# Values of the dilated attention for four head slots in one pass, two slots' values parked in memory

## The chip, the cores and the metric

The kernel runs on one core of a Trainium2 chip. The metric is the device time of one execution in microseconds (us). Of the kernel before, three runs are known: 2054.96, 2056.84 and 2059.21 us, median 2056.84.

## The reference

Two decoder layers over 1024 tokens of 1024 features, in float32. The first layer normalises its input, projects it, and runs three branches: a gated linear recurrence, a dilated attention, and an attention to 256 memory tokens. The second layer is a sparse attention, and this change does not touch it.

The dilated attention has three groups (dilation 1, 4 and 16) of four heads each, 128 features per head. A query of group g sees keys at stride d. The four heads of one group have the same place in the other groups, a "slot", and a slot's three outputs are mixed by their softmax sums:

```
w = jax.nn.softmax(jnp.stack(lses, axis=0), axis=0)
o = jnp.einsum('gbsh,gbshd->bshd', w, jnp.stack(outs, axis=0).astype(jnp.float32))
```

The values v are a plain projection of the normalised input, with 512 columns per group (four slots of 128).

## The kernel before, in words

Every large product is made exact with three matmuls: both operands are split into a high and a low part (high*high, high*low, low*high). The input lies feature-major in eight chunks of 128 features by 1024 tokens, each as a high and a low tile (`self.xt`, `xh` and `xl`).

Weights come as a stream in an order written out by hand (`self.plan`, filled in `layer1`). Each piece is 512 KB. `w()` (L187) hands out piece i, and before that issues the load of piece i+2 on SP's queue and the split of piece i+1: POOL writes the high part (L215), VectorE the low part (L216). Raw, high and low parts share a ring of six buffers (`NW`), so piece i+1's high part takes the buffer of piece i-1's, and can only be written when the matmuls of piece i-1 are done; the load of piece i+2 takes the buffer of raw piece i, and waits for its split.

`proj` (L223) makes a feature-major product: 48 matmuls of 512 columns per piece, with the weights stationary. Queries and keys are made so, one piece per group and slot, and VectorE brings them out of PSUM (L519) in the group's token order.

The values must be token-major, so `dil_vals` (L602) has the input as the stationary operand. `seq_block` (L560) picks its 128 tokens in the group's order: adjacent columns for group 0, every 4th for group 1, every 8th for group 2. The moving operand is 256 weight columns, the values of two slots. One call does one group and two slots: two pieces of four feature chunks each, and for each piece 2 (PSUM tiles) x 4 (token blocks) x 4 (chunks) x 3 matmuls, so 192 matmuls of 256 columns (L613). Each PSUM tile (two banks, `big`, two of them) collects four token blocks; VectorE scales it and writes one tile per slot (L621). `dil_slot` (L740) calls it for the three groups in slot 0 (for slots 0 and 1) and again in slot 2 (for slots 2 and 3): six calls in all.

Scores, mixing weights and outputs of a slot are side work: generators whose steps are woven in by `tick`, called once per six 512-column matmuls of `proj`, and once per token block in `dil_vals` (16 ticks a call). A slot's scores have 12 steps, the mix 3, the output 14; the preparation of the memory operands has 25 steps at the start and 12 when slot 2 begins. The memory attention takes every second tick while it runs. The steps of the memory branch are counted by `next(extra)`, and `M1`, `M2` say at which count its keys and values are made; `M2` is the start of slot 3.

Working tiles of 4 KB per partition come from one ring of 39 (`NU`): the split input holds 16 of them, the values 6.

Of the kernel before, what the change touches and what calls it, by code (L numbers as in the profile page):

```python
# [31 lines left out]
M1, M2, MS = 8, 30, 2  # L32
# [18 lines left out]
class Trunk:  # L51
# [46 lines left out]
    def psum_layout(self, wide):  # L98
        """Four banks as two tiles of two banks, or as three score banks and a third for transposes."""
        if self.wide is not None:  # L100
            self.bs.close()
        self.wide, self.banks, self.fills = wide, 0, 0
        self.bs = ExitStack()
        self.bp = self.bs.enter_context(self.tc.tile_pool(name=self.n("bp"), bufs=1, space=PSUM))
# [25 lines left out]
    def chain(self):  # L130
        """The instruction just made follows the chain's last one (same engine, order only)."""
        cur = self.nc.cur_f.blocks[-1].instructions[-1]
        if self.chained is not None:
            info = mybir.DependencyInfo(mybir.DependencyClass.NoSync, mybir.DependencyReason.SCHED_ONLY)
            self.tc.add_manual_dep(cur, self.chained, info, reason="order")
        self.chained = cur.name

    def order_allocations(self):
        """Tiles of a shared ring take their buffers in the order in which they are first written."""
        first, pos = {}, {}  # L140
        want = {nm for names in self.rings.values() for nm in names}
        for blk in self.nc.cur_f.blocks:
            for ins in blk.instructions:
                for o in getattr(ins, "outs", ()):
                    bap = getattr(o, "bass_ap", None)
                    nm = getattr(getattr(bap, "tensor", None), "name", None)
                    if nm in want and nm not in first:
                        pos[nm] = len(first)
                        first[nm] = ins
        info = mybir.DependencyInfo(mybir.DependencyClass.NoSync, mybir.DependencyReason.SCHED_ONLY)  # L150
        for names in self.rings.values():
            prev = None
            for nm in sorted(names, key=pos.get):
                cur = first[nm]
                if prev is not None and prev.name != cur.name:
                    self.tc.add_manual_dep(cur, prev.name, info, reason="ring order")
                prev = cur

# [28 lines left out]
    def w(self):  # L187
        """Next piece of the planned weight stream as exact (high, low) parts."""
        i = self.pos
        self.pos += 1  # L190
        self.prefetch(i + 3, i + 2)
        r = self.split_w[i]
        self.split_w[i] = None
        return r
# [28 lines left out]
    def proj(self, x, halves=(0, 1)):  # L223
        """Feature-major product: 128 output features against the tokens of the given halves."""
        w = self.w()
        ps = self.big()
        for k in range(8):
            self.proj_step(ps, w, x, k, halves)
            if x[k][0][0].shape[-1] == 512 or k % 4 == 3:
                self.tick()  # L230
        return ps
# [16 lines left out]
    def rstd_steps(self, ssum, nb, p=None):  # L248
        """Columns 1/sqrt(mean+eps) of nb token blocks from per-feature-lane sums of squares."""
# [39 lines left out]
    def split_x(self, src, k, gcol, cuts):  # L289
        """Gain-scaled split operand of feature chunk k, by token halves."""  # L290
# [10 lines left out]
    def split_halves(self, src, k, gcol):  # L301
        """The same with a buffer of its own for each half."""
# [23 lines left out]
    def mem_prep(self, gcol):  # L326
        """Normalised memory, scaled with a layer's gain and split."""
# [25 lines left out]
    def mem_norm(self, raw):  # L353
        """Rows of the memory tokens' 1/rms, the same for both layers."""
# [39 lines left out]
    def mem_kv(self, gcol):  # L394
        """Split keys and values of one layer: each key part fills both partition halves."""
# [35 lines left out]
    def mem_attn(self, q, kv, done, pause=0):  # L431
        """q: two pairs of split heads [2 parts x 64, tokens], already scaled; done(c, out) takes each output."""
# [75 lines left out]
    def dil_proj(self, x, row, g, sc):  # L508
        """Projection scaled and put into the group's sequence order."""
# [16 lines left out]
    def dil_scores(self, D, g, q, k):  # L526
        """Probability numerators of one group with their minima of -s and sums."""
# [32 lines left out]
    def seq_block(self, t, g, m):  # L560
        """Block m of 128 tokens in a group's sequence order."""
# [7 lines left out]
    def to_seq(self, T, fs, out):  # L569
        """Columns of token blocks brought into the order of the second and third group."""  # L570
# [25 lines left out]
    def dil_cols(self, col):  # L596
        """Columns of the norm's factors in each group's order."""
# [4 lines left out]
    def dil_vals(self, g):  # L602
        """Token-major values of a group for two slots."""
        nc = self.nc
        pss = [self.big(), self.big()]
        for kh in range(2):
            h, l = self.w()
            for i, ps in enumerate(pss):
                for b in range(4):
                    for k in range(4):  # L610
                        xh, xl = (self.seq_block(t, g, 4 * i + b) for t in self.xt[4 * kh + k])
                        for j, (x, w) in enumerate(((xh, h), (xh, l), (xl, h))):
                            nc.tensor.matmul(ps[:, 256 * b:256 * b + 256], x, w[:, k, :],  # L613
                                             start=(kh == k == j == b % 2 == 0), stop=(kh == 1 and k == 3 and j == 2),
                                             skip_group_check=True)
                    self.tick()
                if kh:
                    if i == 0:
                        out = [self.u("dv", F32, (128, 8, 128)) for _ in range(2)]
                    for e, v in enumerate(out):  # L620
                        nc.vector.tensor_tensor(v[:, 4 * i:4 * i + 4, :],  # L621
                                                ps.rearrange("p (b s n) -> p s b n", b=4, s=2)[:, e],
                                                self.dcol[g][:, 4 * i:4 * i + 4, None].to_broadcast([128, 4, 128]),
                                                op=ALU.mult)
        return out

    def dil_mix(self, D):
        """Weights of the three groups' numerators, in each group's own order."""
# [111 lines left out]
    def dil_slot(self, s, x, row, extra):  # L740
# [9 lines left out]
        if s % 2 == 0:  # L750
            self.vals = []
            for g in range(3):
                self.vals.append(self.dil_vals(g))
                next(extra)
                next(extra)
        D["v"] = self.vals
        self.add_side(self.dil_out(D))

# [90 lines left out]
    def z_gate(self, i, x, row):  # L849
        """Output chunk i times silu of its gate, v/2 (1 + tanh(v/2))."""  # L850
# [16 lines left out]
    def layer1(self):  # L867
# [5 lines left out]
        for j in range(36):  # L873
            p, i = divmod(j, 18)
            vals = 6 <= i < 12
            if not vals:
                self.pieces(a["hw_dil"][12 * p + i - 6 * (i >= 12)], tile=None if j else self.u)
            elif i % 2 == 0:
                self.pieces(*(a["hw_dv"][6 * p + i - 6 + t] for t in range(2)))
            if not vals:  # L880
                self.pieces(*mem.get(j, ()))
            elif i % 2:
# [130 lines left out]
    def out_proj(self, order, res, done, last=None):  # L1013
        """Feature-major output chunks with the residual added."""
# [39 lines left out]
    def split_pair(self, half, p):  # L1054
        """Two gated feature chunks of a token half as (high, low) parts."""
# [13 lines left out]
    def out_half(self, res):  # L1069
        """Output chunks of the first token half, the residual, and the final norm."""  # L1070
# [48 lines left out]
    def out_tail(self, res):  # L1119
        """The same for the second half, with the last chunk and the norm by quarters."""  # L1120
# [93 lines left out]
    def nsa_group(self, seg):  # L1214
        """Split key operands of one group for the keys that a token half sees."""
# [65 lines left out]
    def cmp_split(self, t, pcol):  # L1281
        """The compression network's input blocks [(parity, d), position pair, (group, block)], split."""
# [95 lines left out]
    def nsa_cmp(self, it):  # L1378
        """Compressed-branch probabilities (transposed, split) and the block selection."""
# [53 lines left out]
    def nsa_query(self, it):  # L1433
        """Split query operands of eight heads with the position and selection rows."""
# [32 lines left out]
    def nsa_scores(self, W):  # L1467
        """Gated probabilities of one branch for two heads."""
# [44 lines left out]
    def nsa_apply(self, W):  # L1513
        """Transposed, split probabilities of one work; the products follow DELAY batches later."""
# [46 lines left out]
    def seg_load(self, seg):  # L1561
        """Operands of a segment (token half, group) that come from memory."""
# [187 lines left out]
    def z_half(self, ps, row, half, z):  # L1750
        """silu of a projected half: v/2 (1 + tanh(v/2))."""
# [7 lines left out]
    def fill_proj(self, x, row):  # L1759
        """Query and gate projections of the second token half."""  # L1760
# [119 lines left out]
def _layout(i):  # L1880
# [21 lines left out]
    for s in range(4):  # L1902
        for g in range(3):
# [3 lines left out]
            if s % 2 == 0:  # L1907
                b = 5120 + (g * 4 + s) * 128
                v = panel(w, r(b, b + 256))
                dv += [v[:, :4], v[:, 4:]]  # L1910
# [46 lines left out]
```

## Time and profile before

| | |
|---|---|
| median of three runs | 2056.84 us |
| profiled execution, first to last instruction (its span) | 2053.8 us |
| PE (matmul) busy | 1974.9 us, 96% |
| VectorE / ScalarE / GpSimd busy | 57% / 41% / 39% |
| DMA | 129.38 MB, mean 63 GB/s |

No time of the profiled execution is given apart from its span. A row of the profile gives the line of the kernel, the engine, the operation, the tiles (out<-in), the shapes and the count; then the busy time and the mean of one. PE is the matmul, PEld the load of its stationary operand, which has records of its own and runs beside the matmuls. The duration of a matmul is longer than its share of the stream, since matmuls are pipelined: the distance from one start to the next is what a matmul costs.

### The profile page before, as it was taken

The page shows a single profiled execution, that of the slowest core. Times are in us where ns is not written, and L with a number is a line of the kernel's source. Part 1 is how long each engine was busy: PE and PEld are TensorE (multiplying, and loading weights), DVE is VectorE, ACT ScalarE, POOL GpSimd, SP SyncE. Part 2 cuts the span into 40 slices and gives each one's busy share as a digit, 9 for nine tenths or more (in the row PEclk, how much of TensorE's full clock was granted, in tenths as well). Part 3 has the DMA queues.
Part 4 walks back from the last instruction along what each step waited for, and adds up shares of the span by engine and source line. Part 5 has one row for each costly group of instructions (what it writes and reads, how often), then busy time and mean ns, then how long its engine had stood idle before and what let it go on. Part 6 is the DMA issues. An engine that isn't in the chain of part 4 may idle for free. (4 is left out here: it accounts for less than half of the span.)

```text
span 2053.8 us, 28410 instructions
## 1 busy us (share of the span) xinstructions
PE 1974.9 (96%) x10594; PEld 1694.0 (82%) x10594; DVE 1166.5 (57%) x2257; ACT 839.8 (41%) x1780; POOL 810.6 (39%) x929
## 2 busy tenths in 40 slices
PE   8999999999999999999999999999999899998997
PEld 7899988889988777788888987778777788887886
DVE  6421255341133475656125466668778877889964
ACT  4210144220021272332005244246557766788861
POOL 6120112221011444441221533466677565577533
PEclk9999999999999999999999999999999999999999
DMA  4111111111112111113222332322222012311013
GB/s 176 42 32 42 52 31 32 52 32 31 31 42 72 32 41 42 42 44 132 76 72 75 101 121 72 112 72 73 62 83 93 18 52 77 99 54 48 12 47 102
DMA packets 53065, 129.38 MB, mean 63 GB/s; under 512 B 7872, under 2 KB 16576, under 8 KB 52928
## 3 DMA queue, kind: packets, MB, share of 16 engines
q1 hardware_dynamic: 52928, 127.57, 19.6%
q8 instruction: 84, 1.38, 0.3%
q14 instruction: 53, 0.43, 0.1%
HBM read 110.78 MB, written 16.78 MB: 62 GB/s over the span
## 5 line engine op out<-in xcount | busy, mean ns | idle before, releaser
L215 POOL TENSOR_SCALAR wh<-raw 128x1024 fp32r<-128x1024 f32 (+2 forms) x137 | 156.4, 1144 | 728.2 <-PE big L239 287.4
L216 DVE TENSOR_TENSOR wl<-raw,wh 128x1024 fp32r<-128x1024 f32 (+4 forms) x139 | 179.1, 1292 | 200.2 <-POOL wh L215 177.8
L1510 POOL TENSOR_SCALAR P<-P,nden,gates 128x640 f32<-128x640 f32 (+7 forms) x256 | 212.8, 841 | 136.0 <-DVE nden L1507 117.8
L239 PE MATMUL big<-xh,wh 128*128 128x512 f32 x752 | 258.4, 424 | 1.1 <-ACT xh L296 0.6
L239 PE MATMUL big<-xl,wh 128*128 128x512 f32 x752 | 242.8, 399 | 4.0 <-DVE xl L297 4.0
L239 PE MATMUL big<-xh,wl 128*128 128x512 f32 x752 | 234.0, 392 | 0.0
L1504 ACT ACTIVATE P<-P,nden 128x640 f32<-128x640 f32 (+7 forms) x256 | 187.5, 733 | 89.9 <-DVE nden L1502 84.4
L1528 DVE TENSOR_TENSOR pl<-t,ph 128x512 fp32r<-128x512 f32 (+1 forms) x304 | 183.2, 614 | 37.2 <-ACT ph L1527 33.5
L1523 PE MATMUL t<-ident,P 128*128 128x128 f32 x1056 | 167.8, 278 | 16.7 <-DVE pl L1528 13.6
L1527 ACT ACTIVATE ph<-t 128x512 fp32r<-128x512 f32 (+1 forms) x304 | 159.3, 533 | 58.8 <-PE t L1523 47.9
L239 PEld LDWEIGHTS big<-xl,wh 128*128 128x128 f32 x752 | 142.0, 189 | 35.3 <-DVE xl L297 5.4
L1523 PEld LDWEIGHTS t<-ident,P 128*128 128x128 f32 x1056 | 126.4, 142 | 50.5 <-DVE pl L1528 12.4
L239 PEld LDWEIGHTS big<-xh,wl 128*128 128x128 f32 x752 | 142.0, 189 | 30.4
L239 PEld LDWEIGHTS big<-xh,wh 128*128 128x128 f32 x752 | 135.2, 190 | 36.6 <-issue 15.1
L239 PE MATMUL big<-x,wh 128*128 128x512 f32 x480 | 144.4, 395 | 0.0
L613 PE MATMUL big<-wh,xh 128*128 128x256 f32 x384 | 140.5, 366 | 0.5 <-DVE kbd L411 0.5
L613 PE MATMUL big<-wl,xh 128*128 128x256 f32 x384 | 139.8, 364 | 0.0
L613 PE MATMUL big<-wh,xl 128*128 128x256 f32 x384 | 139.7, 364 | 0.0
L1549 PE MATMUL acc<-ph,nv 128*128 128x256 f32 x528 | 128.2, 310 | 6.0 <-ACT ph L1527 5.4
L1549 PE MATMUL acc<-pl,nv 128*128 128x256 f32 x528 | 122.3, 299 | 0.0
L1502 DVE CUSTOM_DVE_ANT_0 P<-big,mask 128x640 f32<-128x640 f32 (+3 forms) x128 | 116.7, 913 | 4.0 <-PE big L1493 2.5
L613 PEld LDWEIGHTS big<-wh,xh 128*128 128x128 f32 x384 | 109.7, 286 | 0.9 <-issue 0.7
(339 smaller groups left out, 4321.1 us busy)
## 6 DMA issues: line engine op xcount, KB each, us to landing
raw<-nw_f SPq DMA_DIRECT2D x42, 512.0 KB, 3.6
raw<-hw_dil SPq DMA_DIRECT2D x22, 512.0 KB, 3.6
raw<-now SPq DMA_DIRECT2D x32, 256.0 KB, 2.7
raw<-hw_z SPq DMA_DIRECT2D x14, 512.0 KB, 3.5
raw<-how SPq DMA_DIRECT2D x16, 448.0 KB, 3.4
raw<-hw_dv SPq DMA_DIRECT2D x12, 512.0 KB, 3.6
raw<-hw_xa SPq DMA_DIRECT2D x8, 512.0 KB, 3.6
res<-xT SPq DMA_DIRECT2D x8, 512.0 KB, 5.2
```

Of the source, the lines that this page charges most:

```text
L215: e.tensor_scalar(h[:, k0:k1], raw[:, k0:k1], 1.0, 0.0, op0=ALU.mult, op1=ALU.add)
L216: nc.vector.tensor_tensor(l[:, k0:k1], raw[:, k0:k1], f32(h[:, k0:k1]), op=ALU.subtract)
L239: self.nc.tensor.matmul(o, w[:, k, :], v, start=(k == 0 and i == 0), stop=(k == 7 and i == 2))
L613: nc.tensor.matmul(ps[:, 256 * b:256 * b + 256], x, w[:, k, :], start=(kh == k == j == b % 2 == 0), stop=(kh == 1 and k == 3 and j == 2), ...
L1502: nc.vector.tensor_tensor_reduce(ev, sv, mv, scale=1.0, scalar=3e38, op0=ALU.add, op1=ALU.min, accum_out=den[:, 0, h:h + 1])
L1504: nc.scalar.activation(e, e, AF.Exp, bias=den[:, 0, h:h + 1], scale=-1.0, accum_out=den[:, 1, h:h + 1])
L1510: nc.gpsimd.tensor_scalar(es[h], es[h], den[:, 2, h:h + 1], gt[:, 2 - br, hh:hh + 1], op0=ALU.mult, op1=ALU.mult)
L1523: nc.tensor.transpose(t[:, 256 * i + 128 * h:256 * i + 128 * h + 128], W["e"][h][:, 128 * k:128 * k + 128], self.ident)
L1527: nc.scalar.activation(ph[:, :w], t[:, :w], AF.Copy)
L1528: nc.vector.tensor_tensor(pl[:, :w], t[:, :w], f32(ph[:, :w]), op=ALU.subtract)
L1549: nc.tensor.matmul(o, V[:, k0 + k, :], x[:, 256 * i:256 * i + 256], start=False, stop=(br == 1 and k == nb - 1 and x is pl), skip_group_ch ...
```

## The change

`dil_vals` now does one group for all four slots: 512 moving columns (a whole bank) per token block, two token blocks per PSUM tile. A call makes two passes i over four token blocks each. A pass goes through four weight pieces of two feature chunks x 512 columns, so each piece is loaded and split twice per call. VectorE takes 256 elements per instruction out of PSUM, four instructions after every second block. Slots 0 and 1 go to tiles as before, slots 2 and 3 to a tile `late`, which is stored to memory at the end of the pass. The calls are made in slot 0 only; in slot 2, six loads bring the parked values back. `M2` is 24 in place of 30, which is again the start of slot 3. Docstrings and comments were taken out as well.

```
-        pss = [self.big(), self.big()]
-        for kh in range(2):
-            h, l = self.w()
-            for i, ps in enumerate(pss):
+        out = [self.u("dv", F32, (128, 8, 128)) for _ in range(2)]
+        for i in range(2):
+            pss = [self.big(), self.big()]
+            late = self.u("dvl", F32, (128, 2, 4, 128))
+            for q in range(4):
+                h, l = self.w()
                 for b in range(4):
-                    for k in range(4):
-                        xh, xl = (self.seq_block(t, g, 4 * i + b) for t in self.xt[4 * kh + k])
+                    ps = pss[b // 2][:, 512 * (b % 2):512 * (b % 2) + 512]
+                    for k in range(2):
+                        xh, xl = (self.seq_block(t, g, 4 * i + b) for t in self.xt[2 * q + k])
                         for j, (x, w) in enumerate(((xh, h), (xh, l), (xl, h))):
-                            nc.tensor.matmul(ps[:, 256 * b:256 * b + 256], x, w[:, k, :],
+                            nc.tensor.matmul(ps, x, w[:, k, :], start=(q == k == j == 0),
+                                             stop=(q == 3 and k == 1 and j == 2))
                     self.tick()
+                    if q == 3 and b % 2:
+                        m = 4 * i + b - 1
+                        pv = pss[b // 2].rearrange("p (b s n) -> p s b n", b=2, s=4)
+                        rows = self.dcol[g][:, m:m + 2, None].to_broadcast([128, 2, 128])
+                        for e in range(4):
+                            o = out[e][:, m:m + 2, :] if e < 2 else late[:, e - 2, b - 1:b + 1, :]
+                            nc.vector.tensor_tensor(o, pv[:, e], rows, op=ALU.mult)
+            nc.sync.dma_start(self.dvd[g, i], late)
...
+    def dil_vals_load(self):
+        vals = []
+        for g in range(3):
+            out = [self.u("dv", F32, (128, 8, 128)) for _ in range(2)]
+            for e, t in enumerate(out):
+                self.nc.sync.dma_start(t.rearrange("p (i b) n -> p i b n", i=2),
+                                       self.dvd[g, :, :, e].rearrange("i p b n -> p i b n"))
+            vals.append(out)
+        return vals
...
-        if s % 2 == 0:
+        if s == 0:
+            self.dvd = self.dr.tile([3, 2, 128, 2, 4, 128], F32, name="dvd")
             self.vals = []
             for g in range(3):
                 self.vals.append(self.dil_vals(g))
                 next(extra)
                 next(extra)
+        elif s == 2:
+            self.vals = self.dil_vals_load()
...
+            elif j % 2 == 0:
+                self.pieces(*(a["hw_dv"][2 * (j - 6) + t % 4] for t in range(8)))
```

## Rows read from the trace of the kernel before

**Rows 1.** The page: busy time, share and instructions of each engine.
```profile
PE 1974.9 (96%) x10594; PEld 1694.0 (82%) x10594; DVE 1166.5 (57%) x2257; ACT 839.8 (41%) x1780; POOL 810.6 (39%) x929
```
**Rows 2.** Stretches in us: length, busy time (instructions) by engine, clock, DMA share, GB/s.
```profile
108.00:119.00 11.00, 11.00 (x90) 10.63 (x88) 5.80 (x33) 4.56 (x18) 0.00 (x0) 1.00 0.00 0
142.00:164.00 22.00, 22.00 (x96) 22.00 (x95) 2.52 (x3) 0.00 (x0) 0.91 (x1) 1.00 0.08 25
...
438.00:460.00 22.00, 21.34 (x165) 20.15 (x164) 10.59 (x50) 6.67 (x27) 6.19 (x13) 1.00 0.08 25
...
513.00:536.00 23.00, 23.00 (x97) 23.00 (x96) 2.41 (x3) 0.00 (x0) 0.87 (x2) 1.00 0.08 24
```
**Rows 3.** Line 613 in slot 2, groups 0, 1, 2: duration min/median/max, first and last start.
```profile
L613 PEld LDWEIGHTS big<-wl,xh x64: 187/192/193, 440.1 to 467.6; 128*128 128x128 f32 x64
...
L613 PEld LDWEIGHTS big<-wl,xh x64: 329/329/330, 468.1 to 512.2; 128*128 128x128 f32 x64
...
L613 PE MATMUL big<-wh,xh x64: 393/396/397, 468.0 to 512.1; 128*128 128x256 f32 x64
...
L613 PEld LDWEIGHTS big<-wl,xh x64: 335/338/341, 512.9 to 558.5; 128*128 128x128 f32 x64
...
L613 PE MATMUL big<-wh,xh x64: 399/405/408, 512.8 to 558.4; 128*128 128x256 f32 x64
```
**Rows 4.** Timeline, PE, group 0: start, us, instruction; seven matmuls apart.
```profile
452.84 0.28 PE L613 MATMUL big<-wh,xh 128*128 128x256 f32 x1
...
453.68 0.28 PE L613 MATMUL big<-wl,xh 128*128 128x256 f32 x1
```
**Rows 5.** Timeline, PE, 512-column matmuls of a projection; twelve apart.
```profile
560.03 0.62 PE L239 MATMUL big<-xh,wl 128*128 128x512 f32 x2
...
562.76 0.62 PE L239 MATMUL big<-xh,wl 128*128 128x512 f32 x2
```
**Rows 6.** Timeline, the first two loads of group 2, after an idle PE.
```profile
171.24 0.31 PEld L613 LDWEIGHTS big<-wh,xh 128*128 128x128 f32 x1 [0.71 <-issue]
...
171.45 0.34 PEld L613 LDWEIGHTS big<-wl,xh 128*128 128x128 f32 x1
```
**Rows 7.** Waits: engine, line, who was waited for: us in total, times, longest.
```profile
POOL wh L215 <- PE big L613: 172.3, 10, 22.9
...
PE big L239 <- DVE wl L216: 1.1, 1, 1.1
```
**Rows 8.** Lines, 0 to 500 us: busy, mean ns of one, idle before.
```profile
L216 DVE TENSOR_TENSOR wl<-raw,wh 128x1024 fp32r<-128x1024 f32 (+2 forms) x37 | 45.5, 1229 | 74.0 <-POOL wh L215 73.9
L215 POOL TENSOR_SCALAR wh<-raw 128x1024 fp32r<-128x1024 f32 (+1 forms) x35 | 37.5, 1072 | 290.6 <-PE big L239 107.7 <-PE big L613 106.7 <-issue 50.8
L547 PE MATMUL t<-df,df 128*128 128x128 f32 (+1 forms) x144 | 36.8, 339 | 1.4 <-DVE dst L550 1.0 <-DVE df L519 0.5
L553 ACT ACTIVATE de<-de,dst 128x128 f32<-128x128 f32 (+1 forms) x72 | 32.4, 450 | 49.6 <-DVE dst L550 48.5 <-DVE dnat L639 0.6
L519 DVE SCALAR_TENSOR_TENSOR df<-big,row 128x1024 f32<-128x1024 f32 x17 | 29.4, 1734 | 51.8 <-PE big L239 46.0 <-ACT row L286 5.7
...
L550 DVE CUSTOM_DVE_ANT_0 de<-t,db 128x128 f32<-128x128 f32 (+1 forms) x72 | 25.1, 351 | 37.9 <-PE t L547 37.4
...
L445 DVE TENSOR_TENSOR mpt<-t,mpt 128x256 fp32r<-128x256 f32 x32 | 13.6, 423 | 11.4 <-ACT mpt L444 10.9
...
L621 DVE TENSOR_TENSOR dv<-big,dc 128x512 f32<-128x512 f32 x8 | 5.2, 685 | 38.7 <-PE big L613 38.7
```
**Rows 9.** DMA issues: count, KB each, median us to landing.
```profile
raw<-hw_dv SPq DMA_DIRECT2D x12, 512.0 KB, 3.6
...
q<-qd SPq DMA_DIRECT2D x4, 512.0 KB, 5.7
```
**Rows 10.** SP's own waits: who was waited for, us in total, times, longest.
```profile
SPq L201 <- DVE wl L216: 971.1, 101, 23.0
```

More of the change, by code (lines that the diff above doesn't have):

```diff
@@ L31 @@
 ZST = 4
-M1, M2, MS = 8, 30, 2
+M1, M2, MS = 8, 24, 2
 DAHEAD = 4
@@ L612, in dil_vals @@
                         for j, (x, w) in enumerate(((xh, h), (xh, l), (xl, h))):
-                            nc.tensor.matmul(ps[:, 256 * b:256 * b + 256], x, w[:, k, :],
-                                             start=(kh == k == j == b % 2 == 0), stop=(kh == 1 and k == 3 and j == 2),
-                                             skip_group_check=True)
+                            nc.tensor.matmul(ps, x, w[:, k, :], start=(q == k == j == 0),
+                                             stop=(q == 3 and k == 1 and j == 2))
@@ L616, in dil_vals @@
                     self.tick()
[L617 to L624, printed above, removed]
@@ L872, in layer1 @@
         mem.update({M1 + 3 + i: [a["hw_qm"][i]] for i in range(2)})
-        for j in range(36):
-            p, i = divmod(j, 18)
-            vals = 6 <= i < 12
+        for j in range(30):
+            vals = 6 <= j < 12
             if not vals:
[L877 to L880, printed above, removed]
+                self.pieces(a["hw_dil"][j - 6 * (j >= 12)], tile=None if j else self.u)
                 self.pieces(*mem.get(j, ()))
-            elif i % 2:
+            elif j % 2 == 0:
+                self.pieces(*(a["hw_dv"][2 * (j - 6) + t % 4] for t in range(8)))
+            else:
                 self.pieces(*mem.get(j - 1, ()), *mem.get(j, ()))
@@ L1906, in _layout @@
                 dil.append(panel(w, r(b, b + 128)))
[L1907 to L1910, printed above, removed]
+    for g in range(3):
+        v = panel(w, r(5120 + 512 * g, 5632 + 512 * g))
+        dv += [v[:, 2 * i:2 * i + 2] for i in range(4)]
     a["hw_dil"], a["hw_dv"] = C(np.stack(dil)), C(np.stack(dv))
```

## The prediction

> **What bounds the kernel now.** First the engines' busy times: PE has 1974.9 of 2053.8 us, the next engine 57% [rows 1]. [...] In the stretches of groups 1 and 2 the weight loads are busy without a gap too (22.00 of 22.00, 23.00 of 23.00), while VectorE has 3 instructions and ScalarE none. So the value stage is bound by PE alone; the question is whether by streaming or by loading.
>
> Third, line 613 by group, from one matmul's start to the next. In group 0: 453.68 - 452.84 = 0.84 us for seven, 0.120 us each [rows 4]. In group 1 the 64 high-high matmuls (every third) start between 468.0 and 512.1: 44.1/63/3 = 0.2333 us. In group 2 45.6/63/3 = 0.2413 us [rows 3]. The instructions are of the same shape, 256 moving columns, so streaming cannot be the difference. The loads are: 192 ns in group 0 (adjacent tokens), 329 ns where every 4th token is read, 338 ns for every 8th [rows 3]. A load lasting 0.33 us begins every 0.233 us: part of each record is a tail, the rest stands end to end. Groups 1 and 2 are bound by loading, and half the array's time is unused.
>
> Fourth, what 512 columns cost with a cheap load: 562.76 - 560.03 = 2.73 us for twelve, 0.2275 us [rows 5]. Going from 256 to 512 columns adds 0.2275 - 0.120 = 0.1075 us, and the load of 0.19 us hides in both.
>
> **The change part by part.** Loads and matmuls of line 613 fall from 1152 (six calls of 192) to 576 (three of 192), at 512 columns each. Per group there were 384 and will be 192.
>
> - Group 0: 384 x 0.120 = 46.1 us becomes 192 x 0.2275 = 43.7 us: -2.4 us.
> - Groups 1 and 2: if a load runs wholly beside the stream before it, the step is the longer of the two. 0.2333 and 0.2413 are both above 0.2275, so the step stays and the count halves: 192 x 0.2333 = 44.8 us and 192 x 0.2413 = 46.3 us saved: -91.1 us.
>
> Together -93.5 us. A stream twice as long could slow a load beside it. The first load of group 2 found the array idle and took 0.31 us, the second, with 256 columns beside it, 0.34 us [rows 6]. That gives at most 0.03 us per load for 256 more columns, 384 x 0.03 = 11.5 us; some of this is the second load waiting in line, as it starts before the first is through. I take 0 and keep 11.5 us for the range. Below zero it can't go: the step would have to fall under the load.
>
> [...]
>
> Weight stream: 24 pieces in place of 12, each for 24 matmuls (5.5 to 5.8 us). 12 more loads of 3.6 us [rows 9], 12 x 1.07 us on POOL and 12 x 1.23 us on VectorE [rows 8]. All of it is beside PE, if it fits in a piece's time. Piece i+1's split starts when piece i-1's matmuls end and takes 1.07 + 1.23 = 2.3 us; before, POOL waited for PE there up to 22.9 us and PE almost never for a split (1.1 us) [rows 7]. A load waits for the split two pieces back: 3.6 + 2.3 = 5.9 us per two pieces, against 11 us. What covers it is 3 us per piece; where VectorE is later than that, PE stops. In group 0, where the scores are woven in, VectorE is busy 5.80 of 11 us [rows 2] with two drains in it; another split and a few drains per 8 us still fit. Cost 0.
>
> Drains: 48 of 256 elements in place of 24 of 512: nearest row 0.42 us for 128x256 out of PSUM, against 0.685 us: 20 in place of 16 us [rows 8]. The last four of a pass (1.7 us) lie ahead of a split on VectorE (done at 1.7 + 1.2 = 2.9 us of 5.5), and the second PSUM tile is needed again after 12 matmuls, 2.7 us. Cover 1 us; six times, and once for the query-key drain of 1.73 us before the first call. Between 0 and 6 x 0.5 us; I take 1.5 us.
>
> Stores: six of 512 KB on SP. Each waits for the last drain, some 2 us into the next pass, and the next piece's load stands behind it. That load would else have gone out at 2.3 us into the piece before: it lands at about 2 + 3.6 = 5.6 us, just when its split wants it, and that split has a whole piece of slack. Cost 0; without the slack 6 x 2 = 12 us.
>
> Loads back in slot 2: six, at 3.6 to 5.7 us each (the second for a load of what the kernel had stored) [rows 9], at most 34 us if one by one. Slot 3's weights are behind them on SP. SP runs ahead: on 101 occasions it stood waiting for a split with the next load in hand, 23.0 us at the longest [rows 10]. A projection's piece lasts 48 x 0.2275 = 10.9 us, and a load goes out nearly two pieces before its split. I take 0; the bound is 34 + 3.6 + 2.3 - 21.8 = 18 us, which also stands for waits on the 39 tiles (six more held at once while slot 2's scores still run).
>
> Ticks: 96 in both kernels, but all now in slot 0. Before, in 142 to 164 us and 513 to 536 us nothing was woven in (VectorE has 3 instructions there) [rows 2], so these ticks were empty. By the step counts, slots 2 and 3 keep 96 ticks of their projections, for 70 steps of their own and 14 left of slot 1, and 21 steps stay open at the end of slot 3 before and after. Cost 0.
>
> Sum: 2053.8 - 93.5 + 1.5 = 1961.8 us of span. The median of the runs shown is 3.0 us above the span: 1964.8, said as 1965 us.
>
> **The rivals.**
>
> *Load and stream in series.* If strided loads shut out the stream, the step grows by the 0.1075 us: 0.341 and 0.349 us. 192 x (0.341 + 0.349) = 132.5 us against 182.2 us: -49.7 - 2.4 = -52, so 2005 us. For it: 0.2333 is about 0.107 + 0.126, a load of the usual kind. Against: the loads stand end to end without a gap, and 0.31 us without any stream beside it is nearly 0.34. 5%.
>
> *The weight stream falls behind.* VectorE late by more than 3 us per piece, SP held by the stores (12 us), and the loads back (18 us): 12 to 35 us given back, 1977 to 2000 us. For it: half the time per piece, new waits on SP. Against: SP and POOL wait for PE today, not the other way. 14%.
>
> *Side work runs bare (slower).* If the 96 ticks left do not hold the steps of slots 2 and 3, the rest is stepped through without matmuls around it in the recurrence's stage, which waits for its outputs. A scores step alone takes some 2 x 0.35 on VectorE, 2 x 0.45 on ScalarE and 0.34 us on PE, 1.9 us in a row [rows 8]. From 48 bare steps on (91 us) the gain is gone; all 58 of both slots make 110 us, 2057 - 92 + 110 = 2075 us. For it: slot 2 has 48 ticks fewer, and its scores now end in slot 3. Against: the ticks that went were empty. 3%.
>
> *Nothing changes.* If a strided load cost grew with the moving columns to 0.48 us, 576 would cost what 1152 did: 2054 to 2061 us. No row speaks for it. 1%.
>
> **How the numbers follow.** 77% for the forecast (1960 to 1977 us, with up to 11.5 us for slowed loads), 14, 5, 3 and 1% for the rivals. The range of 80% is 1959 to 1983 us. A measurement of this kernel tells about 0.2% (4 us) from no change. Faster takes in the forecast and the first two rivals, 96%; same 1%; slower 3%.
>
> **What would show it.** Line 613 has 576 matmuls of 512 columns, 0.228, 0.233 and 0.241 us apart in the three groups; loads still 329 and 338 ns. PE has no waits on line 216 or on the drains above 1 us each, and the stage has no PE gaps at the passes' ends. No gap at the start of slot 3. Wrong would be: steps of 0.34 us (serial), PE waiting for splits each 5.5 us (stream), or PE idle in the recurrence with side work alone (bare steps).

## The result and the profile after

The changed kernel takes 1969.62 us (1968.65 to 1978.69, four runs), the kernel before 2056.41 us beside it: a ratio of 0.9586, 95% interval 0.9566 to 0.9606. It is 86.8 us faster; 1965 us was forecast, and the range was 1959 to 1983. The profiled execution has a span of 1966.9 us, 86.9 us under that of before.

First the page's line on the engines, which answers to [rows 1]: PE's busy time is 92.5 us less, so its idle time in the span has grown by 5.6 us.

```profile
PE 1882.4 (96%) x10018; PEld 1590.3 (81%) x10018; DVE 1181.5 (60%) x2293; ACT 839.8 (43%) x1780; POOL 826.0 (42%) x941
```

Then stretches inside the value stage (columns as in [rows 2]): scores woven into group 0, group 1, group 2.

```profile
108.00:119.00 11.00, 11.00 (x57) 8.93 (x56) 8.39 (x37) 3.58 (x15) 2.13 (x2) 1.00 0.18 61
142.00:164.00 22.00, 22.00 (x95) 22.00 (x95) 7.08 (x11) 0.00 (x0) 4.22 (x4) 1.00 0.38 120
200.00:223.00 23.00, 23.00 (x96) 23.00 (x96) 7.64 (x12) 0.00 (x0) 4.54 (x5) 1.00 0.35 114
```

In groups 1 and 2 PE and its loads are still busy throughout, with as many instructions per us as before (95 in 22 us), but each now does 512 columns. VectorE has about three times and GpSimd some five times the work that these groups had before, from splits and drains, and DMA moves 120 in place of 25 GB/s; none of it holds PE in these stretches.

The value matmuls (now line 616), group 0 without side work, then groups 1 and 2, answering to [rows 3]:

```profile
L616 PEld LDWEIGHTS big<-wl,xh x8: 187/188/188, 121.9 to 126.6; 128*128 128x128 f32 x8
...
L616 PE MATMUL big<-wh,xh x64: 394/398/401, 140.3 to 184.8; 128*128 128x512 f32 x64
L616 PEld LDWEIGHTS big<-wl,xh x64: 308/310/311, 140.4 to 184.8; 128*128 128x128 f32 x64
...
L616 PE MATMUL big<-wh,xh x64: 397/405/604, 192.5 to 238.8; 128*128 128x512 f32 x64
L616 PEld LDWEIGHTS big<-wl,xh x64: 317/327/340, 192.7 to 238.8; 128*128 128x128 f32 x64
```

Every third matmul is in a row, so the step is 44.5/63/3 = 0.235 us in group 1 and 46.3/63/3 = 0.245 us in group 2 (0.244 without its first): nearly the 0.233 and 0.241 us of before, for twice the columns.

Last, what PE waited for between 85 and 620 us, the three longest waits:

```profile
PE t L725 <- POOL de L704: 2.6, 1, 2.6
...
PE big L616 <- DVE wl L216: 1.6, 1, 1.6
PE t L585 <- DVE dtmp L582: 1.3, 1, 1.3
```

None of them is in the kernel before, whose largest single wait between these marks is 0.6 us. The first and the third stand at the start of slot 3 (ending at 486.8 and 481.9 us), the second in group 0.

To compare variants, the start of the kernel is better left out: the first value matmul comes between 85 and 89 us, from run to run, with the first loads. The stage from there to the recurrence's first gate matmul holds all that the change touches. That matmul's row, in the kernel before, then in the changed one:

```profile
L814 PE MATMUL t<-xc,gw x64: 590/591/697, 706.8 to 868.7; 128*128 128x512 f32 x64
```

```profile
L830 PE MATMUL t<-xc,gw x64: 590/591/697, 621.3 to 783.2; 128*128 128x512 f32 x64
```

Before, 706.8 - 85.9 = 620.9 us; after, 621.3 - 85.0 = 536.3 us: 84.6 us less. "The stage" below is this figure.

### The profile page after: what moved, and what is told of

It reads as the page before. It is cut to its first block, busy times and chain, and to the rows that moved or that the text cites. A ratio compares the mean times of both kernels' runs of the same rounds, so it can differ in the third digit from the quotient of the medians.

```text
span 1966.9 us, 27378 instructions
## 1 busy us (share of the span) xinstructions
PE 1882.4 (96%) x10018; PEld 1590.3 (81%) x10018; DVE 1181.5 (60%) x2293; ACT 839.8 (43%) x1780; POOL 826.0 (42%) x941
## 5 line engine op out<-in xcount | busy, mean ns | idle before, releaser
L215 POOL TENSOR_SCALAR wh<-raw 128x1024 fp32r<-128x1024 f32 (+2 forms) x149 | 169.5, 1139 | 642.1 <-PE big L239 271.6
L216 DVE TENSOR_TENSOR wl<-raw,wh 128x1024 fp32r<-128x1024 f32 (+4 forms) x151 | 194.5, 1292 | 180.7 <-POOL wh L215 158.9
L239 PEld LDWEIGHTS big<-x,wh 128*128 128x128 f32 x480 | 87.8, 188 | 16.4
L1563 PEld LDWEIGHTS acc<-ph,nv 128*128 128x128 f32 x528 | 86.3, 190 | 14.1 <-ACT ph L1541 11.7
L519 DVE SCALAR_TENSOR_TENSOR df<-big,row 128x1024 f32<-128x1024 f32 x23 | 39.9, 1737 | 92.8 <-PE big L239 88.1
L239 PE MATMUL f<-x,wh 128*128 128x512 f32 x288 | 93.5, 402 | 0.0
```

The costliest lines, as they stand in the source:

```text
L215: e.tensor_scalar(h[:, k0:k1], raw[:, k0:k1], 1.0, 0.0, op0=ALU.mult, op1=ALU.add)
L216: nc.vector.tensor_tensor(l[:, k0:k1], raw[:, k0:k1], f32(h[:, k0:k1]), op=ALU.subtract)
L239: self.nc.tensor.matmul(o, w[:, k, :], v, start=(k == 0 and i == 0), stop=(k == 7 and i == 2))
L519: self.nc.vector.scalar_tensor_tensor(ot[:, sl], p.rearrange("p (i r) -> p i r", r=dil), sc, rt[:, sl], op0=ALU.mult, op1=ALU.mult)
L1563: nc.tensor.matmul(o, V[:, k0 + k, :], x[:, 256 * i:256 * i + 256], start=False, stop=(br == 1 and k == nb - 1 and x is pl), skip_group_ch ...
```

## The experiments

**Is it the strided load?** e1 and e2 read adjacent tokens in all groups, in the kernel before and in the changed one.

```
     def seq_block(self, t, g, m):
-        v = t.rearrange("p (i r) -> p r i", r=ORD[g])
...
+        return t[:, 128 * m:128 * m + 128]
```

> The kernel before, with the stationary tokens of all three groups read as adjacent columns; the values of groups 1 and 2 are then in the wrong token order, nothing else changes. If the strided weight load is what the changed kernel halves (my theory), the loads last 0.19 us everywhere, the step of groups 1 and 2 falls from 0.233 and 0.241 us to 0.120 us, and the time by 384 x (0.113 + 0.121) = 90 us, to 1966 us. If the number of instructions or the width of the stream is what counted, the time stays at 2056 us.

> The changed kernel with the same adjacent reads (values of groups 1 and 2 in the wrong token order). Theory: the step of groups 1 and 2 falls only to that of a 512-column stream, 0.2275 us, from 0.235 and 0.244 us: 192 x (0.0075 + 0.0165) = 4.6 us less, 1965 us, so that without strides the change is worth no more than some 2 us. If strided loads still cost the changed kernel more than the stream hides (load and stream partly in series), it gains far more than 5 us here.

e1: 1966.97 us, ratio to before 0.9557 (0.9541 to 0.9573): without the strides the kernel before is as fast as the changed one. Its loads over all three groups, and two of its matmuls in group 2, eight apart:

```profile
L608 PEld LDWEIGHTS big<-wl,xh 128*128 128x128 f32 x384 | 73.5, 191 | 0.2
```

```profile
459.95 0.28 PE L608 MATMUL big<-wl,xh 128*128 128x256 f32 x1
...
460.91 0.28 PE L608 MATMUL big<-wh,xh 128*128 128x256 f32 x1
```

The loads last 0.19 us everywhere and the step is 0.96/8 = 0.120 us in group 2 too. The stage is 89.5 us shorter than before (620.5 - 89.1 = 531.4), for 90 expected. e2: 1969.34 us, 0.9576 (0.9555 to 0.9596), no less than the changed kernel; its stage is 617.8 - 87.2 = 530.6 us, 5.7 us less, for 4.6 expected. So the whole of the gain is in the strided loads, and with adjacent reads the change brings nothing that can be measured (0.9557 against 0.9576).

In these traces every 4th token costs 0.233 us a step [rows 3], and adjacent ones fit in 0.120 us (e1). What makes the strided load longer was not looked into.

**Load alone, or load and stream?** e3 has half the columns in groups 1 and 2 of the kernel before.

```
+                            c = 256 if g == 0 else 128
-                            nc.tensor.matmul(ps[:, 256 * b:256 * b + 256], x, w[:, k, :],
+                            nc.tensor.matmul(ps[:, 256 * b:256 * b + c], x, w[:, k, :c],
```

> The kernel before with 128 moving columns in place of 256 in groups 1 and 2: the values of slots 1 and 3 are left out there, and those of slots 0 and 2 stand in for them. Theory (the step is the load): steps still 0.233 and 0.241 us, time within 4 us of 2056. Serial rival: each step falls by half of 0.1075 us, 768 x 0.054 = 41 us, to 2015 us.

The steps are as expected: here group 2 in slot 2, 43.9/61/3 = 0.240 us.

```profile
L614 PE MATMUL big<-wh,xh x62: 440/445/447, 519.8 to 563.7; 128*128 128x128 f32 x62
```

The time is not: 2066.4 us in the one run, 2057.64 for the kernel before beside it. The stretches show why:

```profile
142.00:164.00 22.00, 22.00 (x95) 22.00 (x95) 2.51 (x3) 0.00 (x0) 1.05 (x1) 0.50 0.08 25
...
217.50:260.00 42.50, 42.50 (x230) 37.94 (x230) 12.79 (x13) 8.17 (x11) 5.25 (x5) 0.90 0.20 58
...
514.00:560.00 46.00, 46.00 (x194) 46.00 (x193) 4.93 (x6) 0.00 (x0) 2.09 (x2) 0.50 0.07 24
560.00:600.00 40.00, 40.00 (x236) 35.77 (x236) 9.62 (x15) 9.18 (x15) 3.14 (x3) 0.91 0.13 40
```

With 128 columns the granted clock fell to 0.50 while PE and its loads were busy without a gap; with 256 columns it had stayed at 1.00 [rows 2]. The projections that follow paid for it: by the mean clock, an estimate, 42.5 x 0.10 = 4.3 us are lost in 217.5 to 260 us, and 40 x 0.09 = 3.6 us in 560 to 600 us. The whole stage is 714.0 - 86.8 = 627.2 us, 6.3 us longer than before.

The step of 0.240 us at half the clock does not yet tell the two theories apart: if the stream slows with the clock, 128 columns at 0.50 take as long as 256 at 1.00, and load and stream in series would give the same step. What tells is the start of group 1 in slot 2, where the clock was still at 1.00:

```profile
474.00:478.00 4.00, 4.00 (x20) 4.00 (x18) 2.42 (x3) 0.00 (x0) 1.05 (x1) 1.00 0.17 19
```

```profile
474.36 0.40 PE L614 MATMUL big<-wh,xl 128*128 128x128 f32 x1
...
477.86 0.40 PE L614 MATMUL big<-wh,xl 128*128 128x128 f32 x1
```

They are fifteen steps apart: 3.50/15 = 0.2333 us with 128 columns, as with 256 [rows 3]; in series it would be 0.18. So the serial rival is out: at the full clock half the columns took nothing from the step (e3), and twice the columns added 2 to 4 ns (the changed kernel), not 107. The load alone sets the step, and it kept its pace at half the clock: 0.2355 us in group 1 of slot 0 (29 steps from 125.05 to 131.88 us at 0.50).

**Is the parking hidden?** e4 leaves out the six stores and the six loads back, and uses the values of slots 0 and 1 twice.

```
-            nc.sync.dma_start(self.dvd[g, i], late)
...
-            self.vals = self.dil_vals_load()
+            pass
```

> The changed kernel without the six stores and six loads back; slots 2 and 3 use the values of slots 0 and 1, all other work stays. Theory: the parking is hidden, 1968 to 1970 us as the changed kernel, and the two waits of PE at the start of slot 3 (1.3 and 2.6 us) stay. Rival: the loads back (17 us on SP) cause these waits, which then go: 1965 us.

1968.16 us, 0.9567 (0.9553 to 0.9581): by the time alone not to be told from the changed kernel. But both waits at the start of slot 3 are gone (what is left between 440 and 620 us is 0.6 us at most), and the stage is 618.3 - 86.9 = 531.4 us, 4.9 us less. On the waits the rival was right, and the parking, as the changed kernel does it, is not free. The 4.9 us understate it, since in e4 the clock fell at another place, behind the 1.6 us wait for a split in group 0, a wait that left it at 1.00 in the changed kernel:

```profile
136.00:140.00 4.00, 3.10 (x8) 2.40 (x9) 1.99 (x2) 0.00 (x0) 0.00 (x0) 0.64 0.42 140
140.00:144.00 4.00, 4.00 (x18) 3.32 (x17) 1.42 (x4) 0.00 (x0) 0.11 (x1) 0.93 0.34 122
```

That costs e4 some 3.10 x 0.36 + 4 x 0.07 = 1.4 us, by the clock and PE's busy time (an estimate).

**What makes the two waits?** e5 is the changed kernel again, as the base for e6 to e8; e6 makes the second layer's memory keys two projections later.

> The changed kernel as it is, beside the next three on the same chip: 1969 to 1970 us, with a wait of PE of 1.6 us for a split in group 0 of the value stage, and waits of 1.3 and 2.6 us at the start of slot 3.

```
-M1, M2, MS = 8, 24, 2
+M1, M2, MS = 8, 26, 2
```

> The changed kernel with M2 = 26 in place of 24: the keys and values of the second layer's memory attention are made two projections later in slot 3. If the two waits at the start of slot 3 come from the short weight pieces of that product (256 columns, one every 2.9 us) falling together with the mixing weights of slot 2 on VectorE and GpSimd, they go and the time falls by 3.9 us, to 1966 us. Rival: they come from the loads back alone (without the parking they were gone); then they stay and the time stays at 1969 to 1970 us.

e5: 1970.27 us, 0.9578 (0.9565 to 0.9591); waits 1.3 and 2.6 us again, the split's 0.8 us this time. e6: 1966.78 us, 0.9563 (0.9550 to 0.9576), 3.5 us less, though the intervals overlap. The waits did not go; they fell to 0.5 and 1.5 us. So the short pieces of the memory product are a part of it, and neither theory was whole. In the stage e6 is only 0.9 us shorter (620.0 - 86.2 = 533.8 against 620.2 - 85.5 = 534.7 us): most of the 1.9 us of waits saved was lost again to the clock, which stood at 0.50 for 6 us behind them, and for 3 us in e5 (488 to 491 us).

```profile
485.00:491.00 6.00, 6.00 (x23) 4.76 (x23) 0.00 (x0) 2.33 (x3) 5.75 (x16) 0.50 0.00 0
```

e9 moves the six loads behind slot 2's mixing weights, group 2's first; e10 does that and e6.

```
-            self.vals = self.dil_vals_load()
+            self.vals = [None] * 3
+            self.add_side(self.dil_vals_load(self.vals))
...
-        for g in range(3):
+        for g in (2, 0, 1):
...
-            vals.append(out)
-        return vals
+            vals[g] = out
+        return
+        yield
```

> The changed kernel with the six loads back issued as side work after slot 2's mixing weights (group 2's first), in place of before its scores. In the changed kernel they stood 17 us on SP, from 448.4 to 465.1 us, waiting for tiles that slot 2's scores still held. If this early claim on the tiles is what delays the scores and so the mixing at the start of slot 3, the waits of 1.3 and 2.6 us go: 3 to 4 us less than the changed kernel's 1970, so 1966 to 1967 us. Rival: the outputs now wait for the loads themselves (some 5 us to landing): up to 5 us more, 1975 us.

> The same with M2 = 26 as well. If both edits remove the same waits, 1966 us, no better than either alone; if each removes its own part, 1964 us.

e9: 1965.67 us, 0.9550 (0.9535 to 0.9565); both waits are gone, and no wait for the loads came up. Its time is the lowest of all: by the ratios, each to the kernel before on the same chip, it is 0.3% ahead of the changed kernel (e5, 0.9578), with intervals that just touch, and in the stage, at 615.7 - 86.1 = 529.6 us, it is ahead by 5 to 7 us. The clock stays at 1.00 there. e10: 1966.99 us, 0.9558 (0.9540 to 0.9577): no better than e9, so both edits remove the same waits.

What e9 changes can be seen in PE's order at the end of slot 2, where the scores of group 2 (line 547) are woven in. The changed kernel:

```profile
466.33 0.39 PE L547 MATMUL t<-df,df 128*128 128x128 f32 x2
...
471.13 0.39 PE L239 MATMUL big<-xl,wh 128*128 128x512 f32 x1
471.36 0.60 PE L547 MATMUL t<-df,df 128*128 128x128 f32 x4
```

e9:

```profile
467.59 0.60 PE L547 MATMUL t<-df,df 128*128 128x128 f32 x4
468.73 0.38 PE L547 MATMUL t<-df,df 128*128 128x128 f32 x2
469.65 0.39 PE L547 MATMUL t<-df,df 128*128 128x128 f32 x2
```

With the loads ahead of them, 5.0 us (21 projection matmuls) lie between two of these scores; in e9 they come 0.9 to 1.1 us apart. In the changed kernel the mixing that follows then falls together with a projection's drain (L519) and the split of a piece (L216) on VectorE, and its last part (L582) comes behind both:

```profile
477.38 1.21 DVE L519 SCALAR_TENSOR_TENSOR df<-big,row 128x1024 f32<-128x1024 f32 x1
...
478.60 1.21 DVE L216 TENSOR_TENSOR wl<-raw,wh 128x1024 fp32r<-128x1024 f32 x1
...
481.64 0.33 DVE L582 TENSOR_TENSOR dtmp<-df,dc 128x32 f32<-128x32 f32 x2
```

In e9 it comes ahead of both:

```profile
477.12 0.33 DVE L582 TENSOR_TENSOR dtmp<-df,dc 128x32 f32<-128x32 f32 x2
...
478.87 1.22 DVE L519 SCALAR_TENSOR_TENSOR df<-big,row 128x1024 f32<-128x1024 f32 x1
480.13 1.39 DVE L216 TENSOR_TENSOR wl<-raw,wh 128x1024 fp32r<-128x1024 f32 x1
```

So in the changed kernel the weighing (scores times mixing weights, L704) on GpSimd starts 4.5 us later (481.78 against 477.26 us), and PE, by then at the memory keys' short pieces, waits for it.

Is that because tiles are short? On SP the loads stood from 448.4 to 465.1 us. The changed kernel's six, those of e12 (one tile more), and those of e9:

```profile
448.38 17.11 SPq L635 DMA_DIRECT2D dv<-dvd  x6
```

```profile
449.61 7.79 SPq L635 DMA_DIRECT2D dv<-dvd  x6
```

```profile
467.06 3.29 SPq L634 DMA_DIRECT2D dv<-dvd  x6
```

The room for one more large tile (e12) is taken from two tiles of half the size, which have a ring of their own (`NH`), so e11 has that smaller ring alone.

```
-NH = 9
+NH = 7
```

> The changed kernel with 7 in place of 9 half tiles (NH), as the ground for the next run: 1970 us if these two are not needed, a few us more if they are.

```
-NU = 39
+NU = 40
```

> The changed kernel with 7 half tiles and 40 in place of 39 tiles (NU) in the large ring. If the loads back are short of tiles, their stay on SP gets shorter than 17 us, and the waits at the start of slot 3 fall below 3.9 us: some 2 us less than the run with 7 half tiles alone. If tiles are not the cause, the two runs agree.

e11: 1978.09 us, 0.9621 (0.9601 to 0.9641); e12: 1981.5 us, 0.9628 (0.9613 to 0.9644). The half tiles are needed, by 8 us, of which the stage has 1.6 us (623.2 - 85.3 = 537.9 against 536.3). With the 40th tile the loads stood 7.8 us in place of the 17.1 us of e11 and the changed kernel, and both waits stayed at 1.3 and 2.6 us. So the stay on SP does not make the waits: e9's time came out as expected, but not for the reason given there. What does is the place of the loads in the written order, ahead of the scores. (e9 also loads group 2 first; the two were not tried apart.) By which rule the order of the instructions comes out of the written one was not looked into.

**The wait in group 0.** e7 writes the high parts of the value pieces on ScalarE; e8 does that and e6.

```
+                if tuple(raw.shape[1:]) == (2, 512):
+                    nc.scalar.activation(h[:, k0:k1], raw[:, k0:k1], AF.Copy)
+                else:
+                    e.tensor_scalar(h[:, k0:k1], raw[:, k0:k1], 1.0, 0.0, op0=ALU.mult, op1=ALU.add)
-                e.tensor_scalar(h[:, k0:k1], raw[:, k0:k1], 1.0, 0.0, op0=ALU.mult, op1=ALU.add)
```

> The changed kernel with the high parts of the value pieces written by ScalarE (idle in that stage) in place of GpSimd. If the 1.6 us wait in group 0 is a split standing behind twelve weighing instructions on GpSimd (12 x 0.4 us), it goes: 2 us less, 1967 to 1968 us. If it is VectorE's low part that is late by itself, or the load, the wait stays and the time too.

> Both of the last two edits: 1969.6 - 3.9 - 2 = 1964 us if both waits go and nothing else comes up; 1969 us if other waits take their place.

GpSimd in the changed kernel:

```profile
127.62 0.93 POOL L704 TENSOR_SCALAR de<-de,df 128x256 f32<-128x256 f32 x2
128.53 3.25 POOL L704 TENSOR_SCALAR de<-de,dfg 128x128 f32<-128x128 f32 x8
131.74 2.09 POOL L215 TENSOR_SCALAR wh<-raw 128x1024 fp32r<-128x1024 f32 x2
```

The split that could start at about 127 us, when its buffer came free, stood behind ten weighing instructions until 131.7; with only 5.5 us per piece PE ran dry from 133.3 to 134.9. The same weighing stood there before, beside a piece of 22 us. In e7 ScalarE does that split at 130.06 us, and PE's wait is gone. The time is not less: 1971.35 us, 0.9579 (0.9566 to 0.9592), 2 us expected. The stage is 622.4 - 88.0 = 534.4 us, 0.3 to 1.9 us under the two runs of the changed kernel. The clock at the start of slot 3 took part of the gain: it was at 0.50 from 488 to 494 us, twice as long as in e5. e8: 1968.46 us, 0.9570 (0.9557 to 0.9583), 1964 expected; its waits at slot 3 are those of e6 (0.5 and 1.5 us). Gains of this size are too small for these runs.

**What a short wait costs beside itself.** The start of slot 3 in the changed kernel, and in e9 (columns as in [rows 2]):

```profile
484.00:487.00 3.00, 0.40 (x2) 0.17 (x1) 1.57 (x3) 0.14 (x1) 3.00 (x6) 0.89 0.35 97
487.00:491.00 4.00, 4.00 (x14) 2.74 (x15) 0.00 (x0) 1.19 (x2) 4.00 (x12) 0.50 0.14 58
491.00:495.00 4.00, 4.00 (x22) 3.69 (x21) 0.00 (x0) 2.31 (x2) 1.44 (x4) 0.73 0.00 0
```

```profile
485.00:490.00 5.00, 5.00 (x33) 4.34 (x32) 1.61 (x2) 3.01 (x4) 5.00 (x9) 1.00 0.00 0
490.00:495.00 5.00, 5.00 (x36) 4.46 (x35) 0.47 (x2) 1.56 (x3) 1.00 (x3) 1.00 0.35 108
```

After waiting 1.3 and 2.6 us of 7, PE runs at 0.50 for 4 us and at a mean of 0.73 for 4 more: 4 x 0.50 + 4 x 0.27 = 3.1 us lost on top of the 3.9 us. (The 3 us ahead of them are mostly the wait itself, so their clock adds nothing.) In e5 the clock fell for less long (0.62, then 0.96): 4 x 0.38 + 4 x 0.04 = 1.7 us. These are estimates, which take PE's work to go at the pace of the clock; e3 showed that strided loads do not (0.2333 us a step at 1.00, 0.2355 us at 0.50).

## Why the prediction was right, and by how much not

- *The bound.* Right: groups 1 and 2 were bound by their strided loads alone. With adjacent reads their step fell to 0.120 us (e1), and half the columns took nothing from it (e3).
- *Groups 1 and 2, half the loads at the same step.* Right: -91.1 us forecast; the steps grew by 0.002 and 0.003 us, which is 192 x 0.005 = 0.9 us given back, of a bound of 11.5 us. Load and stream in series would have made the steps 0.34 and 0.35 us; the trace shows 0.235 and 0.245 us. The sign "loads still 329 and 338 ns" did not come true, without harm: the records are 310 and 327 ns.
- *Group 0, 0.120 to 0.2275 us.* Right within the rows: eight high-high matmuls in 4.7 us are 0.224 us a step, as near as rows to 0.1 us give it.
- *Drains, 1.5 us at the ends of passes.* Not seen; no wait stands there.
- *Weight stream, cost 0.* Wrong in one piece of 24: 1.6 us (0.8 us in e5), where the sign allowed 1 us. I had counted the split's own 2.3 us and VectorE's lateness, not what stands ahead of it on GpSimd.
- *Stores, cost 0.* Right: no wait of PE has one in it.
- *Ticks, cost 0.* Right as far as bare side work goes: from 620 to 800 us PE is busy for 179.5 of 180 us.
- *Loads back, cost 0, and "no gap at the start of slot 3".* This is the step that failed. I priced the loads as a transfer and a queue (18 us at most, SP running ahead). They did stand 17.1 us on SP, and PE never waited for one; but their place in the written order drew the scores of slot 2 apart and put its mixing onto the memory keys at the start of slot 3. It cost 3.9 us of waits and some 3.1 us of clock. Nothing in the forecast had the clock.

The sum, for the stage: -93.5 + 0.9 + 1.6 + 3.9 + 3.1 = -84.0 us, measured -84.6; for e5 -93.5 + 0.9 + 0.8 + 3.9 + 1.7 = -86.2, and 534.7 - 620.9 = -86.2 measured; for e9, without the slot 3 terms, -91.0, and -91.3 measured. So the stage missed its forecast of -92.0 us by 7.4 us. The terms give 8.0: 7.0 us at the start of slot 3, 1.6 for the split and 0.9 for the steps, less the 1.5 us that I had put at the passes' ends. The span missed by only 5.1 us (86.9 in place of 92.0), since 0.9 us were gained ahead of the stage and 1.4 us behind it. No run shows that the change did that, and the runs of one kernel differ by more; so these 2.3 us are luck.

## What to carry to other kernels

Where the stationary operand is read with a stride, compare the distance between matmuls with that of the same shape and adjacent reads; here it was 0.233 and 0.241 us against 0.120 us, the load was the bound, and 256 more moving columns per load added only 2 to 4 ns. A phase made twice as fast halves the time in which its helpers may be late: look at what else stands on their queues, not only at how long their own work takes. Put reloads next to their readers, not ahead of work that has no use for them.

## What was not expected of the hardware

- The strided weight load kept its pace when the clock was at half: in group 1 of e3, 0.2333 us a step at 1.00 and 0.2355 us at 0.50.
- PE and its loads 100% busy did not hold the clock: with 128 columns per 0.24 us step it fell to 0.50 (e3), with 256 it stayed at 1.00 [rows 2].
- Waits of 1.3 and 2.6 us within 7 us were followed by a clock of 0.50, from 487 to 493 us in the changed kernel and from 488 to 491 us when the same kernel ran again (e5). Waits of 0.5 and 1.5 us were followed by 0.50 from 485 to 491 us (e6). What sets the length stays open.
- The step of group 2 at 512 columns, its first matmul left out, was 0.244 us in the changed kernel and 0.246 us in e5, the same kernel; what makes the difference stays open.
